# A two-layer hybrid encoder on one core: earlier weight loads, squares summed on VectorE, alternating output tiles, turned weights copied by ScalarE

## The chip, the core and the metric

The kernel runs on one core of a Trainium2 chip. The core has five engines with a queue each: PE (TensorE, matmuls and transposes), DVE (VectorE), ACT (ScalarE), POOL (GpSimd) and SP (SyncE, which here issues nearly all DMAs). PE writes its results to PSUM, which is handed out in banks of 128x512 float32; the other operands lie in SBUF. The metric is the device time of one execution in microseconds (us); less is better.

## The reference

Two layers over x of 512 tokens by 1024. Layer 0 mixes tokens by differential attention, layer 1 by chunked gated linear attention; both also attend to 256 tokens of memory with 4 heads, and each layer ends with a feed-forward part with a causal convolution of width 3.

```python
def rms_norm(x, g):
    xf = x.astype(jnp.float32)
    y = xf * lax.rsqrt(jnp.mean(xf * xf, axis=-1, keepdims=True) + EPS)
    return (y * g.astype(jnp.float32)).astype(x.dtype)
...
def memory_cross_attention(q, mem, mem_norm_g, w_kv, qk_norm_g):
    ...
    kv = rms_norm(mem, mem_norm_g) @ w_kv
    k, v = jnp.split(kv, 2, axis=-1)
    ...
    logits = jnp.einsum('bqhd,bkhd->bhqk', q, k).astype(jnp.float32)
    p = jax.nn.softmax(logits, axis=-1)
    o = jnp.einsum('bhqk,bkhd->bqhd', p.astype(v.dtype), v)
    return o.reshape(B, S, MEM_WIDTH)

def conv_ffn(h, w_up, conv_w, conv_b, w_down):
    u = h @ w_up
    c = lax.conv_general_dilated(u, ...) + conv_b
    a, g = jnp.split(c, 2, axis=-1)
    return (jax.nn.silu(g) * a) @ w_down
...
    for i in range(DEPTH):
        h = rms_norm(x, attn_norm[i])
        ...
        mix = diff_attention(...)   or   gla_attention(...)
        cross = memory_cross_attention(mem_q, mem, mem_norm[i], w_mem_kv[i], mem_qk_norm[i])
        x = x + jnp.concatenate([mix, cross], axis=-1) @ w_out[i]
        h = rms_norm(x, ffn_norm[i])
        x = x + conv_ffn(h, w_up[i], conv_w[i], conv_b[i], w_down[i])
    return x
```

## The kernel before

**Precision.** Every product of two float32 matrices is made of three matmuls in the faster format fp32r. Each operand is split in a high part (`xh`, `whi`: rounded to fp32r by ACT) and a low part (`xl`, `wlo`: what the rounding lost, by DVE); the products high x high, high x low and low x high add up in one PSUM bank. So each block of weights costs one ACT cast (`split_weights`, L199) and one DVE difference (L200), and each tile of activations one ACT scaling (L226) and one DVE instruction (L227).

**Weights.** All weights are packed in the order of their use into "pieces" of one or more blocks of 128 x up to 1024 (512 KB). `make_piece` (L202) loads a block into one of three `raw` buffers and splits it into one of five `whi` and five `wlo` buffers (WB). `weights(key)` (L216) hands out the next piece and makes pieces until the one after it is also made.

**Activations.** x is held transposed as eight tiles of 128 x 512, one for each 128 of the 1024 features (KT = 8; k counts them). A pool of 40 tiles of that size (`xtile`) serves all intermediate results. PSUM has four tags (`mm`, `sm`, `lg`, `tp`) with two banks each. A bank can be taken again only when the engine that reads its result is done.

**Order.** PE runs in program order. The start block (L336 to L395) also fixes the order of ACT, DVE, POOL and SP by hand; elsewhere a scheduler places the instructions of these four. Each engine works its queue off strictly in order, so an instruction that waits holds up all behind it. SP's DMAs go over eight lanes in turn; a DMA waits until the one eight places before it has landed.

**The start.** Eight times a tile of x and half a block of weights are loaded; `operands(k)` splits them and sums the squares of x (`squares`, L322: ACT squares, the sum is added by POOL, the last one by DVE). The first product (queries and keys of the first heads, `("qk", 0)`) takes them as they come, 12 matmuls for each k into four banks (L391 to L395). At k = 4 two small matmuls make the rows of the relative bias (`bias_rows`, copied to `bs` by DVE, L307). At k = 6 `weights` is called, which makes the second piece of four blocks (issues its loads, casts and differences); `token_rsqrt` forms the norm from the summed squares by a small matmul (L332), a logarithm and an exponential on ACT, and a Newton step on DVE (L175 to L177); then come the loads of constants, memory (`memT`), the vector of column factors (`cols`) and others. After the start, `small_vectors` scales seven of the columns on DVE (L400 to L403). The results of the first product are scaled out of PSUM by ACT (`qs`, `ks`, L539 and L540), and PE goes on with the second piece (L243 to L245).

**Attention with memory.** `MemAttn` runs in both layers beside the token mixer. For each of 8 units (4 token blocks x 2 halves of the heads): logits (L470), the negated maximum on DVE (L473), the exponential on ACT (L477), `turn` (four PE transposes into a `tp` bank, copied to SBUF by DVE, L487), `values` (L499). In layer 0 these steps lie in slots between the units of the differential attention, and matmuls of the big products (`Filler`) fill the gaps in PE's order.

**Out-projection.** `PASS` (L36) lists parts; each part is a list of (column block c, feature tiles ks). A column block is 256 wide and gives two output tiles 2c and 2c+1 (n = 0, 1). `unit` (L933) issues three matmuls for each ks into an `mm` bank; after the last, `update` (L922) adds the bank to x on DVE (L923); in the last part of a layer it also splits the new x for the feed-forward part and sums its squares (POOL, the last by DVE). In the last part of layer 0, blocks 2 and 3 have four ks (12 matmuls a tile), blocks 0 and 1 two (6 matmuls); their order is 2, 0, 1, 3.

**Feed-forward.** For each q, `up` (L954) makes four products: up and gate weights, n = 0 and 1; each sums over all eight k in their natural order (`product`, L255). DVE and ACT do the convolution (L961) and the gate. `("dn", ...)` goes back to 1024, again through `update`; at the end of layer 0 that also splits and sums squares.

Of the kernel before, what the change touches and what calls it, by code (L numbers as in the profile page):

```python
# [20 lines left out]
KT = D // 128  # L21
# [9 lines left out]
WB = 5  # L31
# [5 lines left out]
         [(2, (6, 7, 4, 5)), (0, (4, 5)), (1, (4, 5)), (3, (6, 7, 4, 5))]],  # L37
# [90 lines left out]
def trunk(ctx, tc, x_t, mem_t, wpack, cols_a_d, cols_d, conv_d, gate_d, rel_bias, diff_lambda, consts, onehot, out):  # L128
# [73 lines left out]
    def make_piece():  # L202
        parts = []
        for _, _, kk, _, w in blocks[len(made)]:
            n = len(kk)
            raw = wp.tile([128, WTILE], F32, name="raw", tag="raw", bufs=3)[:, :n * w]
            hi, lo = (wp.tile([128, WTILE], F32R, name=t, tag=t, bufs=WB)[:, :n * w] for t in ("whi", "wlo"))
            nc.sync.dma_start(raw, wpack[at[0], :, :n * w])
            split_weights(slice(0, n * w), raw, hi, lo)
            at[0] += 1  # L210
            parts += [(hi[:, blk(j, w)], lo[:, blk(j, w)]) for j in range(n)]
        made.append(parts)
# [42 lines left out]
    def product(p, parts, n, pairs, ids=None):  # L255
        for i in range(len(parts)) if ids is None else ids:
            (hi, lo), (bh, bl) = parts[i], pairs[i]
            mm(p, hi[:, blk(n)], bh, start=i == 0, stop=False)  # L258
            mm(p, hi[:, blk(n)], bl, start=False, stop=False)  # L259
            mm(p, lo[:, blk(n)], bh, start=False, stop=i == len(parts) - 1)  # L260
# [41 lines left out]
    def bias_rows(rb, oh, bs):  # L302
        for c in (slice(0, 512), slice(512, 640)):
            n = c.stop - c.start
            p = bank("lg")
            mm(p[:6, :n], rb, oh[:, c], start=True, stop=True)
            V.tensor_copy(bs[:, c], p[:6, :n])  # L307
# [14 lines left out]
    def squares(src, acc, on_dve):  # L322
        sq = xtile()
        A.activation(sq, src, AF.Square)
        if acc[0] is not None:
            (V if on_dve else G).tensor_add(sq, sq, acc[0])
        acc[0] = sq
# [7 lines left out]
    E = mybir.EngineType  # L335
    with tc.tile_pool(name="ini", bufs=1) as ip, tc.manual_schedule(engines={E.Activation, E.DVE, E.Pool, E.SP}):  # L336
# [3 lines left out]
        bs = ip.tile([6, 640], F32, name="bs")  # L340
        lv = perm.tile([128, 256], F32, name="lv")
        load = nc.sync.dma_start
# [15 lines left out]
        load(oh, onehot)  # L358
        parts, acc, split_w = [], [None], [None]
        made.append(parts)  # L360

        def operands(k):
            if k % 2 == 0:
                split_w[0] = [wp.tile([128, WTILE], F32R, name=n, tag=n, bufs=WB) for n in ("whi", "wlo")]
            c = blk(k % 2, S)
            hi, lo = split_w[0]
            xh[k], xl[k] = split_tiles()
            split(xh[k], xl[k], xT[k], c_attn(0, k))
            split_weights(c, raws[k // 2], hi, lo)
            parts.append((hi[:, c], lo[:, c]))  # L370
            squares(xT[k], acc, k == KT - 1)

        operands(0)
        for k in range(KT):
            if k + 1 < KT:
                operands(k + 1)
            if k == 4:
                bias_rows(rb, oh, bs)
            if k == KT - 2:
                weights(("qk", 0))  # L380
                token_rsqrt("lg", acc[0], NB, r_x[:, 0])
                load(bias_d, bs)
                load(C[:, 0:640], consts[:, 0:640])
                for i in range(4):
                    load(memT[i], mem_t[i])
                load(cols, cols_d)
                load(lv, diff_lambda[0].rearrange("a b -> (a b)").partition_broadcast(128))
                for l in range(2):
                    load(cv[l].rearrange("p a b -> p (a b)"), conv_d[l])
                load(gw, gate_d)  # L390
            hi, lo = parts[k]  # L391
            for b in range(NB):
                mm(first[b], xh[k][:, blk(b)], hi, start=k == 0, stop=False)
                mm(first[b], xh[k][:, blk(b)], lo, start=False, stop=False)
                mm(first[b], xl[k][:, blk(b)], hi, start=False, stop=k == KT - 1)  # L395

# [10 lines left out]
    def mem_squares():  # L407
        for i in range(4):
            squares(memT[i], mem_acc, False)
        sq = mem_acc[0]  # L410
        G.tensor_add(sq[:, 0:256], sq[:, 0:256], sq[:, 256:512])
# [35 lines left out]
    class MemAttn:  # L447
# [33 lines left out]
        def turn(self, u):  # L481
            pe, sm = self.live[u]
            pt = bank("tp")
            for t in range(4):
                transpose(pt[:, blk(t)], pe[:, blk(t)])
            pT = xtile()
            V.tensor_copy(pT, pt)  # L487
            self.live[u] = pT, sm
# [433 lines left out]
    def update(n, p, gain, acc):  # L922
# [5 lines left out]
        squares(xT[n], acc, n == KT - 1)  # L928

    def out_proj(l, mix, part, acc):  # L930
        got = {}

        def unit(c, ks, n, i):  # L933
            if i == 0:
                if n == 0:
# [6 lines left out]
        for c, ks in PASS[l][part]:  # L942
            for n in range(2):
                for i in range(len(ks)):
                    F.add(0.65, lambda c=c, ks=ks, n=n, i=i: unit(c, ks, n, i))

    def ffn(pool, l, acc):
# [4 lines left out]
        nu = [0]  # L952

        def up(parts, n):  # L954
# [3 lines left out]
            product(p, parts, n, list(zip(xh, xl)))  # L958
# [143 lines left out]
```

## Time and profile before

| | us |
|---|---|
| runs | 1226.18, 1223.9, 1224.32 (median 1224.32) |
| profiled execution | 1225.72 |
| its span | 1223.5 |
| PE busy | 1206.7 (99%) |
| DVE busy | 759.5 (62%) |
| ACT busy | 536.5 (44%) |
| POOL busy | 47.4 (4%) |
| summed squares on POOL (L326) | 42.0 in 27 instructions |
| differences of weights on DVE (L200) | 247.9 in 215 instructions |
| turned weights copied by DVE (L487) | 11.0 in 16 instructions |
| granted PE clock | 1.00 |

The profile describes one execution. The busy share of an engine is the time in which it had an instruction at work. In lists of single instructions the first two columns are start and duration in us; a bracket at the end gives the idle time of the engine before the instruction and the instruction that ended it ("<-DVE xt L923": it waited for DVE's instruction of line 923 that writes an `xt`). In the list of waits the columns are the waiting instruction, what it waited for, the sum in us, how often, and the longest. In the table of stretches each engine has its busy time and its count of instructions. Engine names with a q (SPq) are the queue itself, where a DMA is issued. A chain is followed back from the last instruction, at each step to what released it.

### The profile page before, as it was taken

The page shows a single profiled execution, that of the slowest core. Times are in us where ns is not written, and L with a number is a line of the kernel's source. Part 1 is how long each engine was busy: PE and PEld are TensorE (multiplying, and loading weights), DVE is VectorE, ACT ScalarE, POOL GpSimd, SP SyncE. Part 2 cuts the span into 40 slices and gives each one's busy share as a digit, 9 for nine tenths or more (in the row PEclk, how much of TensorE's full clock was granted, in tenths as well). Part 3 has the DMA queues.
Part 4 walks back from the last instruction along what each step waited for, and adds up shares of the span by engine and source line. Part 5 has one row for each costly group of instructions (what it writes and reads, how often), then busy time and mean ns, then how long its engine had stood idle before and what let it go on. Part 6 is the DMA issues. An engine that isn't in the chain of part 4 may idle for free.

```text
span 1223.5 us, 15052 instructions
## 1 busy us (share of the span) xinstructions
PE 1206.7 (99%) x5818; PEld 979.9 (80%) x5818; DVE 759.5 (62%) x1233; ACT 536.5 (44%) x901; POOL 47.4 (4%) x52
## 2 busy tenths in 40 slices
PE   9999999999999999999999999999999999999998
PEld 6777777778888888888887887888788888888887
DVE  6567578887777435777444436677867662376741
ACT  6666666554434213444436333435544332243420
POOL 3010000030000000000110000002100000000000
PEclk9999999999999999999999999999999999999999
DMA  6432231232322332323341221133323232232231
GB/s 234 145 106 95 78 113 52 70 119 71 105 102 86 103 104 87 103 85 104 114 130 52 69 70 57 40 121 129 104 69 118 89 106 88 83 113 94 83 116 43
DMA packets 39365, 117.76 MB, mean 96 GB/s; under 512 B 4679, under 2 KB 5720, under 8 KB 39294
## 3 DMA queue, kind: packets, MB, share of 16 engines
q1 hardware_dynamic: 39150, 116.79, 29.3%
q8 instruction: 45, 0.74, 0.2%
q14 instruction: 26, 0.21, 0.0%
q10 hardware_dynamic: 144, 0.02, 0.0%
HBM read 112.58 MB, written 4.21 MB: 95 GB/s over the span
## 4 chain that ended last, share of the span: by engine, by line
PE 90%; DVE 4%; ACT 2%; DMA 2%; issue 1%; SPq 0%; ACTq 0%; DVEq 0%
PE ps_mm L258 8%; PE ps_mm L259 8%; PE ps_mm L260 8%; PE ps_sm L258 7%; PE ps_sm L259 7%; PE ps_sm L260 6%; PE ps_mm L243 6%; PE ps_mm L245 6%; PE ps_mm L244 6%; PE ps_tp L258 3%; PE ps_tp L259 3%; PE ps_tp L260 3%; PE ps_lg L259 3%; PE ps_lg L260 3%; PE ps_lg L258 3%; PE ps_tp L168 2%
## 5 line engine op out<-in xcount | busy, mean ns | idle before, releaser
L199 ACT CAST whi<-raw 128x1024 fp32r<-128x1024 f32 (+4 forms) x215 | 209.2, 975 | 275.4 <-PE ps_tp L259 133.7
L200 DVE TENSOR_TENSOR wlo<-raw,whi 128x1024 fp32r<-128x1024 f32 (+4 forms) x215 | 247.9, 1155 | 119.7 <-ACT whi L199 115.9
L258 PE MATMUL ps_mm<-xsh,whi 128*128 128x512 f32 x480 | 190.7, 397 | 2.7 <-DVE xt L923 2.7
L259 PE MATMUL ps_mm<-xsl,whi 128*128 128x512 f32 x480 | 187.4, 390 | 0.0
L260 PE MATMUL ps_mm<-xsh,wlo 128*128 128x512 f32 x480 | 187.3, 390 | 0.0
L243 PE MATMUL ps_mm<-whi,xsh 128*128 128x512 f32 (+2 forms) x352 | 138.1, 392 | 2.7 <-ACT ks L540 2.7
L258 PE MATMUL ps_sm<-xsh,whi 128*128 128x512 f32 x352 | 137.1, 389 | 0.0
L260 PE MATMUL ps_sm<-xsh,wlo 128*128 128x512 f32 x352 | 137.0, 389 | 0.0
L259 PE MATMUL ps_sm<-xsl,whi 128*128 128x512 f32 x352 | 137.0, 389 | 0.0
L245 PE MATMUL ps_mm<-whi,xsl 128*128 128x512 f32 (+2 forms) x352 | 131.5, 374 | 0.3 <-DVE xsl L227 0.3
L244 PE MATMUL ps_mm<-wlo,xsh 128*128 128x512 f32 (+2 forms) x352 | 130.7, 371 | 0.0
L964 ACT ACTIVATE cvo<-u,cv 128x512 f32<-128x512 f32 x88 | 71.6, 814 | 121.3 <-DVE u L962 121.3
L258 PEld LDWEIGHTS ps_mm<-xsh,whi 128*128 128x128 f32 x480 | 90.2, 188 | 23.6 <-DVE xt L923 3.2
L260 PEld LDWEIGHTS ps_mm<-xsh,wlo 128*128 128x128 f32 x480 | 90.1, 188 | 19.0
L259 PEld LDWEIGHTS ps_mm<-xsl,whi 128*128 128x128 f32 x480 | 90.2, 188 | 18.6 <-DVE xsl L227 0.6
L965 DVE SCALAR_TENSOR_TENSOR cvo<-u,cv,cvo 128x512 f32<-128x512 f32 x88 | 65.9, 749 | 38.5 <-ACT cvo L964 38.5
L243 PEld LDWEIGHTS ps_mm<-whi,xsh 128*128 128x128 f32 x352 | 66.3, 188 | 17.6 <-issue 4.7
L260 PEld LDWEIGHTS ps_sm<-xsh,wlo 128*128 128x128 f32 x352 | 66.1, 188 | 13.7
L258 PEld LDWEIGHTS ps_sm<-xsh,whi 128*128 128x128 f32 x352 | 66.1, 188 | 13.7
L259 PEld LDWEIGHTS ps_sm<-xsl,whi 128*128 128x128 f32 x352 | 66.1, 188 | 13.6
L245 PEld LDWEIGHTS ps_mm<-whi,xsl 128*128 128x128 f32 x352 | 66.2, 188 | 12.8 <-DVE xsl L227 0.5
L244 PEld LDWEIGHTS ps_mm<-wlo,xsh 128*128 128x128 f32 x352 | 66.6, 189 | 9.4
(232 smaller groups left out, 1802.2 us busy)
## 6 DMA issues: line engine op xcount, KB each, us to landing
raw<-in_wpack_dram SPq DMA_DIRECT2D x176, 512.0 KB, 3.6
raw<-in_wpack_dram SPq DMA_DIRECT2D x28, 256.0 KB, 2.6
xt<-in_x_t_dram SPq DMA_DIRECT2D x16, 256.0 KB, 5.6
xres<-xt SPq DMA_DIRECT2D x8, 256.0 KB, 3.6
xt<-xres SPq DMA_DIRECT2D x8, 256.0 KB, 4.0
out_dram<-xt SPq DMA_DIRECT2D x8, 256.0 KB, 2.0
bt<-bias_d SPq DMA_DIRECT2D x6, 256.0 KB, 3.5
raw<-in_wpack_dram SPq DMA_DIRECT2D x4, 384.0 KB, 2.9
```

The source lines that it names most:

```text
L168: nc.tensor.transpose(dst, src, ident[:n, :n])
L199: A.copy(hi[:, c], raw[:, c])
L200: V.tensor_sub(lo[:, c], raw[:, c], hi[:, c].bitcast(F32))
L243: mm(p, sh[k][:, blk(b)], hi, start=k == 0, stop=False)
L244: mm(p, sh[k][:, blk(b)], lo, start=False, stop=False)
L245: mm(p, sl[k][:, blk(b)], hi, start=False, stop=k == KT - 1)
L258: mm(p, hi[:, blk(n)], bh, start=i == 0, stop=False)
L259: mm(p, hi[:, blk(n)], bl, start=False, stop=False)
L260: mm(p, lo[:, blk(n)], bh, start=False, stop=i == len(parts) - 1)
L964: A.activation(c, u[:, 2:], AF.Identity, scale=cv[l][:, 2, j:j + 1], bias=cv[l][:, 3, j:j + 1])
L965: V.scalar_tensor_tensor(c, u[:, 1:S + 1], cv[l][:, 1, j:j + 1], c, op0=ALU.mult, op1=ALU.add)
```

## The change

Five things are changed.

1. At the start, the loads of the second piece's four blocks are issued directly behind those of the first: three into the `raw` buffers, the fourth into the start's own buffer `raws[0]` after k = 0 has been read from it. `make_piece` then takes the buffers that it is given. The loads of constants, memory and columns stand behind the start block and outside the order by hand, as does what follows them; only the store of the bias rows stays in it, in two parts from two tiles.
2. All sums of squares are added by DVE: at the start, for the memory (L407), in the out-projections, and at the end of layer 0's feed-forward part.
3. The last part of layer 0's out-projection takes blocks in the order 2, 0, 3, 1, and `tiles` gives the output tiles in the order 4, 0, 5, 1, 6, 2, 7, 3: a tile of 12 matmuls, then one of 6.
4. The products of layer 0's up-projection sum over k in the same order; layer 1 keeps the natural one.
5. `turn` copies with ACT where DVE did.

```diff
@@ -34,7 +34,7 @@
 C4 = tuple(range(4))
 
 PASS = ([[(c, (0, 1)) for c in C4], [(c, (2, 3)) for c in C4], [(c, (6, 7)) for c in (0, 1)],
-         [(2, (6, 7, 4, 5)), (0, (4, 5)), (1, (4, 5)), (3, (6, 7, 4, 5))]],
+         [(2, (6, 7, 4, 5)), (0, (4, 5)), (3, (6, 7, 4, 5)), (1, (4, 5))]],
         [[(c, (0, 1, 2, 6, 7)) for c in C4], [(c, (3, 4, 5)) for c in C4]])
 
 
@@ -199,15 +199,21 @@
         A.copy(hi[:, c], raw[:, c])
         V.tensor_sub(lo[:, c], raw[:, c], hi[:, c].bitcast(F32))
 
-    def make_piece():
+    def raw_tile():
+        return wp.tile([128, WTILE], F32, name="raw", tag="raw", bufs=3)
+
+    def load_raw(raw, n):
+        nc.sync.dma_start(raw[:, :n], wpack[at[0], :, :n])
+        at[0] += 1
+        return raw
+
+    def make_piece(raws=None):
         parts = []
-        for _, _, kk, _, w in blocks[len(made)]:
+        for i, (_, _, kk, _, w) in enumerate(blocks[len(made)]):
             n = len(kk)
-            raw = wp.tile([128, WTILE], F32, name="raw", tag="raw", bufs=3)[:, :n * w]
-            hi, lo = (wp.tile([128, WTILE], F32R, name=t, tag=t, bufs=WB)[:, :n * w] for t in ("whi", "wlo"))
-            nc.sync.dma_start(raw, wpack[at[0], :, :n * w])
+            raw = load_raw(raw_tile(), n * w) if raws is None else raws[i]
+            hi, lo = (wp.tile([128, WTILE], F32R, name=t, tag=t, bufs=WB) for t in ("whi", "wlo"))
             split_weights(slice(0, n * w), raw, hi, lo)
-            at[0] += 1
             parts += [(hi[:, blk(j, w)], lo[:, blk(j, w)]) for j in range(n)]
         made.append(parts)
 
@@ -253,11 +259,13 @@
 
 
     def product(p, parts, n, pairs, ids=None):
-        for i in range(len(parts)) if ids is None else ids:
+        ids = range(len(parts)) if ids is None else ids
+        first, last = (ids[0], ids[-1]) if len(ids) == len(parts) else (0, len(parts) - 1)
+        for i in ids:
             (hi, lo), (bh, bl) = parts[i], pairs[i]
-            mm(p, hi[:, blk(n)], bh, start=i == 0, stop=False)
+            mm(p, hi[:, blk(n)], bh, start=i == first, stop=False)
             mm(p, hi[:, blk(n)], bl, start=False, stop=False)
-            mm(p, lo[:, blk(n)], bh, start=False, stop=i == len(parts) - 1)
+            mm(p, lo[:, blk(n)], bh, start=False, stop=i == last)
 
 
     xT = [None] * KT
@@ -304,7 +312,7 @@
             n = c.stop - c.start
             p = bank("lg")
             mm(p[:6, :n], rb, oh[:, c], start=True, stop=True)
-            V.tensor_copy(bs[:, c], p[:6, :n])
+            V.tensor_copy(bs[c.start // 512], p[:6, :n])
 
     def lam(lv, lp):
         l2 = small("l2")[:, :2]
@@ -319,11 +327,11 @@
     memT = [xtile() for _ in range(4)]
     first = [bank("mm"), bank("mm"), bank("sm"), bank("sm")]
 
-    def squares(src, acc, on_dve):
+    def squares(src, acc):
         sq = xtile()
         A.activation(sq, src, AF.Square)
         if acc[0] is not None:
-            (V if on_dve else G).tensor_add(sq, sq, acc[0])
+            V.tensor_add(sq, sq, acc[0])
         acc[0] = sq
 
     def token_rsqrt(tag, sq, nb, y, on_dve=False):
@@ -333,13 +341,13 @@
         return rsqrt(p[:, :nb], nb, 1.0 / D, on_dve, y=y)
 
     E = mybir.EngineType
+    load = nc.sync.dma_start
     with tc.tile_pool(name="ini", bufs=1) as ip, tc.manual_schedule(engines={E.Activation, E.DVE, E.Pool, E.SP}):
         idle = ip.tile([128, 512], F32, name="idle")
         rb = ip.tile([32, 6], F32, name="rb")
         oh = ip.tile([32, 640], F32, name="oh")
-        bs = ip.tile([6, 640], F32, name="bs")
+        bs = xtile()[:6], xtile()[:6, :128]
         lv = perm.tile([128, 256], F32, name="lv")
-        load = nc.sync.dma_start
         A.dma_start(cols_a, cols_a_d)
         G.memset(idle, 0.0)
         p = bank("tp")
@@ -356,6 +364,7 @@
         load(C[:, 640:768], consts[:, 640:768])
         load(rb, rel_bias)
         load(oh, onehot)
+        second = [load_raw(raw_tile(), WTILE) for _ in range(3)]
         parts, acc, split_w = [], [None], [None]
         made.append(parts)
 
@@ -368,31 +377,36 @@
             split(xh[k], xl[k], xT[k], c_attn(0, k))
             split_weights(c, raws[k // 2], hi, lo)
             parts.append((hi[:, c], lo[:, c]))
-            squares(xT[k], acc, k == KT - 1)
+            squares(xT[k], acc)
 
         operands(0)
         for k in range(KT):
             if k + 1 < KT:
                 operands(k + 1)
+            if k == 0:
+                second.append(load_raw(raws[0], WTILE))
             if k == 4:
                 bias_rows(rb, oh, bs)
             if k == KT - 2:
+                make_piece(second)
                 weights(("qk", 0))
                 token_rsqrt("lg", acc[0], NB, r_x[:, 0])
-                load(bias_d, bs)
-                load(C[:, 0:640], consts[:, 0:640])
-                for i in range(4):
-                    load(memT[i], mem_t[i])
-                load(cols, cols_d)
-                load(lv, diff_lambda[0].rearrange("a b -> (a b)").partition_broadcast(128))
-                for l in range(2):
-                    load(cv[l].rearrange("p a b -> p (a b)"), conv_d[l])
-                load(gw, gate_d)
+                for c in range(2):
+                    load(bias_d[:, 512 * c:min(512 * c + 512, 640)], bs[c])
             hi, lo = parts[k]
             for b in range(NB):
                 mm(first[b], xh[k][:, blk(b)], hi, start=k == 0, stop=False)
                 mm(first[b], xh[k][:, blk(b)], lo, start=False, stop=False)
                 mm(first[b], xl[k][:, blk(b)], hi, start=False, stop=k == KT - 1)
+
+    load(C[:, 0:640], consts[:, 0:640])
+    for i in range(4):
+        load(memT[i], mem_t[i])
+    load(cols, cols_d)
+    load(lv, diff_lambda[0].rearrange("a b -> (a b)").partition_broadcast(128))
+    for l in range(2):
+        load(cv[l].rearrange("p a b -> p (a b)"), conv_d[l])
+    load(gw, gate_d)
 
     def small_vectors():
         lam(lv, xtile()[:, 0:128].rearrange("p (a b) -> p a b", a=2))
@@ -406,9 +420,9 @@
 
     def mem_squares():
         for i in range(4):
-            squares(memT[i], mem_acc, False)
+            squares(memT[i], mem_acc)
         sq = mem_acc[0]
-        G.tensor_add(sq[:, 0:256], sq[:, 0:256], sq[:, 256:512])
+        V.tensor_add(sq[:, 0:256], sq[:, 0:256], sq[:, 256:512])
 
 
     def mem_kv(l):
@@ -484,7 +498,7 @@
             for t in range(4):
                 transpose(pt[:, blk(t)], pe[:, blk(t)])
             pT = xtile()
-            V.tensor_copy(pT, pt)
+            A.copy(pT, pt)
             self.live[u] = pT, sm
 
         def values(self, u):
@@ -925,24 +939,31 @@
             return
         xh[n], xl[n] = split_tiles()
         split(xh[n], xl[n], xT[n], gain(n))
-        squares(xT[n], acc, n == KT - 1)
+        squares(xT[n], acc)
+
+
+    def tiles(l, part):
+        cs, kk = [c for c, _ in PASS[l][part]], dict(PASS[l][part])
+        if l == 0 and part == 3:
+            return [2 * c + n for a in (0, 2) for n in range(2) for c in cs[a:a + 2]], kk
+        return [2 * c + n for c in cs for n in range(2)], kk
 
     def out_proj(l, mix, part, acc):
         got = {}
 
         def unit(c, ks, n, i):
             if i == 0:
-                if n == 0:
+                if c not in got:
                     got[c] = weights(("o", l, part, c))
                 got["p"] = bank("mm")
             p = got["p"]
             product(p, got[c], n, [mix[k] for k in ks], (i,))
             if i == len(ks) - 1:
                 update(2 * c + n, p, None if acc is None else (lambda k: c_ffn(l, k)), acc)
-        for c, ks in PASS[l][part]:
-            for n in range(2):
-                for i in range(len(ks)):
-                    F.add(0.65, lambda c=c, ks=ks, n=n, i=i: unit(c, ks, n, i))
+        todo, kk = tiles(l, part)
+        for n in todo:
+            for i in range(len(kk[n // 2])):
+                F.add(0.65, lambda n=n, i=i: unit(n // 2, kk[n // 2], n % 2, i))
 
     def ffn(pool, l, acc):
         rB = pool.tile([128, S], F32, name="rB", bufs=1)
@@ -950,12 +971,13 @@
         for u in us:
             G.memset(u[:, 0:2], 0.0)
         nu = [0]
+        order = tiles(l, len(PASS[l]) - 1)[0]
 
         def up(parts, n):
             i = nu[0]
             nu[0] += 1
             p = bank("mm" if i % 4 < 2 else "sm")
-            product(p, parts, n, list(zip(xh, xl)))
+            product(p, parts, n, list(zip(xh, xl)), order)
             return p, us[i % 4]
 
         def conv(p, u, j):
```

## The prediction

> **What bounds the kernel now.** I read the page first (busy shares, then the chain that ended last), then the list of waits for PE, then a table of stretches, and last the order of single instructions wherever PE waits.
>
> ```profile
> span 1223.5 us, 15052 instructions
> PE 1206.7 (99%) x5818; PEld 979.9 (80%) x5818; DVE 759.5 (62%) x1233; ACT 536.5 (44%) x901; POOL 47.4 (4%) x52
> PE 90%; DVE 4%; ACT 2%; DMA 2%; issue 1%; SPq 0%; ACTq 0%; DVEq 0%
> ```
>
> PE is busy for 1206.7 of 1223.5 us and holds 90% of the chain. The change leaves PE the same matmuls, so what it can win lies in the 16.8 us in which PE is idle; what it can lose has no such bound, because every us by which an operand comes late is a us of the end.
>
> ```profile
> PE ps_mm L258 <- DVE xt L923: 2.7, 3, 1.0
> PE ps_mm L243 <- ACT ks L540: 2.7, 1, 2.7
> PE ps_tp L168 <- DVE xt L487: 1.1, 1, 1.1
> PE ps_sm L499 <- DVE xt L487: 0.9, 1, 0.9
> ```
>
> These four waits (7.4 us: sum, number, longest) are the ones that the change touches directly: three waits for the add of the out-projection (L923), one at the start for the first keys, two for the copy of the turned weights (L487).
>
> ```profile
> 0.00:31.60 31.60, 29.88 (x114) 20.95 (x114) 22.01 (x24) 18.67 (x29) 9.53 (x11) 1.00 0.70 239
> 31.60:60.00 28.40, 25.72 (x128) 20.97 (x128) 13.73 (x44) 17.50 (x42) 0.29 (x2) 1.00 0.39 134
> 150.00:250.00 100.00, 96.67 (x584) 77.11 (x583) 78.66 (x206) 57.68 (x159) 0.14 (x1) 1.00 0.24 77
> 276.00:608.00 332.00, 331.95 (x1460) 273.63 (x1459) 208.79 (x258) 131.32 (x162) 4.42 (x3) 1.00 0.31 97
> 838.00:866.00 28.00, 26.99 (x118) 21.21 (x117) 23.14 (x27) 18.78 (x26) 11.29 (x10) 1.00 0.35 114
> ```
>
> Columns: stretch, length, busy time of PE, PEld, DVE, ACT, POOL, granted clock, DMA share, GB/s. The feed-forward stretch 276 to 608 has no idle PE at all; 331.95/1460 gives 0.227 us per 128x512 matmul, the unit of all that follows. The gaps are at the start, in the attention with memory (150 to 250) and around the out-projections.
>
> **The start.** Rows of SP, POOL, DVE and PE, then three of the chain, then the bandwidth of the first 36 us in 40 slices:
>
> ```profile
> 12.59 13.00 SPq L208 DMA_DIRECT2D raw<-in_wpack_dram  x4
> 15.13 3.24 POOL L326 TENSOR_TENSOR xt<-xt 128x512 f32<-128x512 f32 x2 [0.17 <-ACT xt L324]
> 9.01 1.38 DVE L227 SCALAR_TENSOR_TENSOR xsl<-xt,cols_a,xsh 128x512 fp32r<-128x512 f32 x1 [0.33 <-ACT xsh L226]
> 17.14 1.78 DVE L200 TENSOR_TENSOR wlo<-raw,whi 128x512 fp32r<-128x512 f32 x1
> 19.50 0.68 DVE L200 TENSOR_TENSOR wlo<-raw,whi 128x512 fp32r<-128x512 f32 x1
> 20.10 0.87 DVE L307 COPY bs<-ps_lg 6x512 f32<-6x512 f32 x2
> 23.43 0.67 DVE L326 TENSOR_TENSOR xt<-xt 128x512 f32<-128x512 f32 x1
> 24.03 3.48 DVE L200 TENSOR_TENSOR wlo<-raw,whi 128x1024 fp32r<-128x1024 f32 x3
> 30.85 1.23 DVE L200 TENSOR_TENSOR wlo<-raw,whi 128x1024 fp32r<-128x1024 f32 x1 [3.35 <-ACT whi L199]
> 33.87 0.27 DVE L400 TENSOR_SCALAR cols<-cols 128x1 f32<-128x1 f32 x3 [0.61 <-DMA cols<-in_cols_dram]
> 18.30 1.24 PE L306 MATMUL ps_lg<-oh,rb 32*6 32x512 f32 x4
> 13.95 5.73 DMA raw<-in_wpack_dram
> 25.26 4.41 DMA raw<-in_wpack_dram
> 34.32 0.50 PE ps_mm L243
> GB/s 0 2 216 369 180 269 330 316 323 396 401 410 401 389 394 356 308 319 405 401 364 46 0 0 0 0 0 0 18 141 348 304 217 328 394 369 289 200 329 378
> ```
>
> The fourth block of the second piece is issued only at 25.26, when DVE has read the first of the three raw buffers; it takes 4.41 us, and cast, difference, root and evacuation follow it until PE goes on at 34.32 after 2.7 us of idleness. The changed kernel reads that block into a start buffer, behind the third (issued at 13.95, landed at 13.95 + 5.73 = 19.7). At the 400 GB/s of the row its 512 KB take 1.3 us, so it lands at about 21.0. Squares added by DVE cost 0.67 less 0.07 of overlap, 0.60 each, but DVE's differences fall from 1.78 to 0.68 once POOL adds nothing beside them.
>
> That would be the whole 2.7, were it not for the order of DVE. Seven scalings of the columns vector (L400 to L403 of before) now stand in DVE's queue behind the square add of k=5 and ahead of the bias rows' copies and of all operands of k=6 and 7. DVE gets there early: from 9.0, where it starts on k=2, four steps of 1.86 (0.66 + 0.60 + 0.60) and the left-over add bring it to about 17. But the columns' load stands on SP behind the fourth block and the 320 KB of constants: 21.0 + 0.8 + a few tenths for the small transfer itself, T = 22.2. From T: 0.5 for the scalings, 0.8 for the copies, 2 x 1.86 for the operands, which makes T + 5.0 = 27.2 for the last square add. PE waits for that add with the product for the root, which stands ahead of the matmuls of k=6 and 7. It comes there after the bias rows (19.5 in before) and 24 matmuls (5.4), at 24.9 less the half us that POOL's neighbourhood cost before that: 24.3, so it waits about 3. The four differences of the second piece (3.48/3 = 1.16 each) end at T + 9.7 = 31.9; in before the last one ended at 32.1 and PE went on 2.2 later, so now at 34.1. Against 34.32 this is -0.2. The stall moves from behind the first product to its middle, and the end follows T one for one. Bounds: with T early enough not to matter PE does not wait at 24.3 and has 6.0 of work to the end of the first product, 30.3, which is -4.0; T = 24 gives +1.6. The columns' load in before waits 0.61 behind the other transfers; that speaks for a T with the queue, and I take 22.2. The memory tiles and the next weights are issued earlier than before, the bias rows go out in two stores behind DVE's copies; their readers have 10 us, so nothing is added.
>
> PE would stand idle for some 3 us. In before it stood for 2.7, and the granted clock in the stretch from 31.6 is 1.00; I add nothing, with 24 x 0.227 = 5.4 as the upper bound (the matmuls of k=6 and 7 at half rate).
> [...]
>
> **The squares of memory.** Four adds move from POOL to DVE in 60 to 150, where PE has under 1 us of waits and none for DVE's sums: 0, bounds -0.3 and +0.3.
>
> **The out-projections.** PE with its wait, DVE in two stretches, and the mean of the add:
>
> ```profile
> 259.29 0.50 PE L258 MATMUL ps_mm<-xsh,whi 128*128 128x512 f32 x1 [0.72 <-DVE xt L923]
> 263.33 0.50 PE L258 MATMUL ps_mm<-xsh,whi 128*128 128x512 f32 x1 [0.98 <-DVE xt L923]
> 260.88 1.79 DVE L227 SCALAR_TENSOR_TENSOR xsl<-xt,cols,xsh 128x512 fp32r<-128x512 f32 x1
> 263.20 0.74 DVE L227 SCALAR_TENSOR_TENSOR xsl<-xt,cols,xsh 128x512 fp32r<-128x512 f32 x1
> 854.20 2.31 DVE L200 TENSOR_TENSOR wlo<-raw,whi 128x1024 fp32r<-128x1024 f32 x1
> ```
>
> In layer 0 the last part has tiles of 12 matmuls (2.72 us) and of 6 (1.36). Per tile DVE has the add 0.60, the low half 0.66 and now the square add 0.60, 1.86 in all, and four differences of 1.16. Two short tiles in a row give DVE 2.72 for 3.72 of work, so PE waits for a bank: 0.72 and 0.98 above. Long and short in turn give 4.08 for 3.72, plus a difference now and then. Followed tile by tile, one wait of 0.9 is left, before the last tile, and the first product of the feed-forward ends at 273.1 instead of 274.5: -1.4. Bounds: both waits gone -1.9; if DVE falls behind by the seven adds (4.2) less the four differences of 1.1 that POOL stretched (1.79 against 0.74) +0.5.
>
> In layer 1 all tiles are alike (9 matmuls, 2.05 us) and the order stays. DVE is busy for 23.1 of 28 us there; seven adds bring 7 x 0.60 = 4.2, and the rows that POOL stretched (2.31 for 1.16 among them) give back about 3.4. DVE needs 1.86 per tile and half a difference of 1.16, 2.4 against PE's 2.05, so PE waits three times for 0.5 to 0.9 where it waited once for 1.0: +1.0, bounds -0.8 and +1.5.
>
> **The turned weights on ACT.** Layer 0, then layer 1, then the nearest row for such a copy on ACT:
>
> ```profile
> 193.74 0.68 DVE L487 COPY xt<-ps_tp 128x512 f32<-128x512 f32 x1
> 194.48 0.66 PE L168 MATMUL ps_tp<-C,ks 128*128 128x128 f32 x4 [1.08 <-DVE xt L487]
> 194.98 0.21 ACT L477 ACTIVATION_READ_ACCUMULATOR xt<-ps_lg,nmm 128x1 f32 x1
> 675.33 1.00 PE L499 MATMUL ps_sm<-vm,xt 128*128 128x64 f32 x8
> 676.03 1.05 ACT L199 CAST whi<-raw 128x1024 fp32r<-128x1024 f32 x1
> 679.06 1.11 PE L499 MATMUL ps_sm<-vm,xt 128*128 128x64 f32 x8 [0.90 <-DVE xt L487]
> L612 ACT COPY xt<-ps_tp 128x512 f32<-128x512 f32 x6 | 3.5, 579 | 0.0
> ```
>
> A copy costs 0.58 on ACT, 0.68 on DVE; what counts is what stands ahead of it. At 194 it is now behind the four exponentials, which end at 195.1: the copy ends at 195.7, PE's keys start then and not at 194.48: +1.2. At 208 a weight cast of 0.6 has moved between the exponentials: +0.5. DVE, 79% busy from 150 to 250, loses eight copies (4.8), from which I expect back 0.6 in the small waits there. In layer 1 the first copy stands behind two casts: it begins at 676.03 + 0.95 = 677.0 and ends at 677.6. Its reader, in before at 675.33, waits 2.3; the wait of 0.90 at 679.06 has its operand early then and goes: +1.4. The other copies come in time by the same reckoning, two of them just so. Sum +2.5; bounds -2.0 (both waits for L487 gone, nothing in their place) and +4.0.
>
> **The sum.** -0.2 + 0 - 1.4 + 1.0 + 2.5 = +1.9. The profiled execution took 1225.72 us, of which 1223.5 are its span, so 1227.6 by its own time. The runs are 1226.18, 1223.9 and 1224.32; the median 1224.32 lies 1.4 under the profiled one, and against it the forecast is 1226.2.
>
> **The rivals.**
> A, faster: the columns land early or PE's wait for them is short, and ACT takes the copies without being late. Start -2, out-projections -1.4 and 0, copies -0.4 (between -2 and +1.2): -3.8, 1220.5. For it: DVE is the busier engine in every stretch with waits, and all four waits quoted go. Against it: the orders of DVE and ACT described above.
> B, slower: T is 24 (+1.8 over the forecast), because the small columns transfer waits as it did in before (0.61 behind its neighbours, 5.3 after its issue at 28.59), or the clock falls in PE's longer idle time. 1228.0. From T = 22.8 on it passes the 0.2% named below.
> C, slower: weights of layer 0's feed-forward come late.
>
> ```profile
> L965 DVE SCALAR_TENSOR_TENSOR cvo<-u,cv,cvo 128x512 f32<-128x512 f32 x88 | 65.9, 749 | 38.5 <-ACT cvo L964 38.5
> ```
>
> Its products take k in the alternated order too, so they need both blocks of a piece at their beginning and hold both to the end. Of five buffers four are live; the time from a freed block to its need falls from two products to one, 24 x 0.227 = 5.4 us. Cast 1.05, difference 1.16 and four of DVE's convolution steps ahead of them (4 x 0.75) make 5.2, just inside. One step more is 0.5 per group of four products, times 11 groups 5.5: 1231.7. Against it: PE loses 0.05 us in 332 now.
>
> **How the numbers follow.** Forecast 0.44, its own range 1224.4 to 1228.0; A 0.30; B 0.14; C 0.12. A difference under 0.2% (1221.9 to 1226.8) can't be told from none. Faster: most of A, 0.27. Slower: B, C and a third of the forecast's case, 0.40. Same: the rest, 0.33. The range reaches to the middle of A and short of C: 1220.5 to 1230.0.
>
> **What would show it.** Start: the DVE row of the first column scaling with a wait for its DMA, ending near 22.2, and PE waiting about 3 us for the last square add, with ks L540 no more among the waits. Out-projection: waits for L923 in layer 0 fall to one, in layer 1 rise to three. Copies: the waits for L487's successor on ACT of 2.3 at 194 and 2.3 at 675. Feed-forward: 332 us with 0 to 0.1 idle, or C is right. The forecast fails if the scalings don't wait, or if ACT's copies end before 194.5 and 675.3.

## The result, and the profile after

The changed kernel takes 1233.9 us (median of five executions, 1231.01 to 1236.94), the kernel before 1225.55 beside it (1223.9 to 1227.06). The ratio is 1.0073, 95% interval 1.006 to 1.0087: 8.35 us slower by the medians, where 1.9 were forecast and the range ended at 1230.0. The profiled execution took 1236.94 and is the slowest of the five; this has to be kept in mind when its numbers are added up. The kernel before, timed again beside the experiments, has medians of 1224.72, 1224.85 and 1226.15 there, so a difference between medians of two experiments can be off by about 1 us.

The page of the changed kernel, its waits for PE, and its stretches (columns as before):

```profile
span 1235.2 us, 15019 instructions
PE 1214.0 (98%) x5818; PEld 984.9 (80%) x5818; DVE 749.6 (61%) x1245; ACT 545.5 (44%) x917; POOL 4.6 (0%) x24
```
```profile
PE ps_lg L340 <- DVE xt L334: 3.0, 1, 3.0
PE ps_sm L513 <- ACT xt L501: 3.0, 2, 2.1
PE ps_mm L266 <- DVE xt L937: 2.5, 5, 0.7
PE ps_tp L168 <- ACT xt L501: 2.3, 1, 2.3
PE ps_lg L601 <- ACT xt L491: 1.6, 4, 0.8
```
```profile
0.00:31.60 31.60, 27.28 (x96) 19.44 (x97) 20.15 (x37) 18.97 (x29) 0.73 (x5) 0.92 0.81 277
31.60:60.00 28.40, 28.40 (x136) 23.06 (x136) 11.17 (x34) 15.56 (x37) 0.29 (x2) 0.97 0.22 74
150.00:250.00 100.00, 94.78 (x564) 75.81 (x562) 68.82 (x185) 59.70 (x162) 0.29 (x2) 0.97 0.21 71
276.00:608.00 332.00, 331.39 (x1454) 272.45 (x1453) 209.42 (x263) 130.46 (x162) 0.00 (x0) 1.00 0.29 97
640.00:710.00 70.00, 66.42 (x372) 53.01 (x370) 26.41 (x59) 36.04 (x84) 0.53 (x1) 0.98 0.21 71
```

The waits for ks L540 (2.7) and for DVE's copies (1.1 and 0.9) are gone, and in their place stand waits of 3.0 at the start, of 2.3 in layer 0 and of 2.1 and 0.9 in layer 1. But for the 0.9, that was the forecast. What was not in its sum is the column of the granted clock: 0.92 and 0.97 at the start, 0.97 and 0.98 in the stretches with the other long waits; before, it was 1.00 in all of these. And PE's busy time rose by 7.3 us for the same 5818 matmuls. So part of the time went not into waiting but into slower matmuls. Two of the three places, in PE's order:

```profile
27.37 1.86 PE L340 MATMUL ps_lg<-C,xt 128*128 128x1 f32 x8 [3.02 <-DVE xt L334]
29.09 0.77 PE L398 MATMUL ps_mm<-whi,xsh 128*128 128x512 f32 x1
29.67 0.63 PE L399 MATMUL ps_mm<-wlo,xsh 128*128 128x512 f32 x1
30.09 0.63 PE L400 MATMUL ps_mm<-whi,xsl 128*128 128x512 f32 x1
...
33.51 0.40 PE L399 MATMUL ps_sm<-wlo,xsh 128*128 128x512 f32 x1
33.74 0.39 PE L400 MATMUL ps_sm<-whi,xsl 128*128 128x512 f32 x1
```
```profile
684.47 1.11 PE L513 MATMUL ps_sm<-vm,xt 128*128 128x64 f32 x8 [2.07 <-ACT xt L501]
685.41 1.03 PE L168 MATMUL ps_tp<-C,xt 128*128 128x128 f32 x4
686.10 0.78 PE L249 MATMUL ps_mm<-whi,xsh 128*128 128x512 f32 x1
686.67 0.63 PE L250 MATMUL ps_mm<-wlo,xsh 128*128 128x512 f32 x1
687.10 0.63 PE L251 MATMUL ps_mm<-whi,xsl 128*128 128x512 f32 x1
```

Behind the wait of 3.02 the matmuls start 0.42 to 0.43 us apart (29.67, 30.09) instead of 0.227, until 33.5. Behind the 2.07 us of idle time in layer 1 it is the same (686.67, 687.10).

### The profile page after: what moved, and what is told of

It reads as the page before. It is cut to its first block, busy times and chain, and to the rows that moved or that the text cites. A ratio compares the mean times of both kernels' runs of the same rounds, so it can differ in the third digit from the quotient of the medians.

```text
span 1235.2 us, 15019 instructions
## 1 busy us (share of the span) xinstructions
PE 1214.0 (98%) x5818; PEld 984.9 (80%) x5818; DVE 749.6 (61%) x1245; ACT 545.5 (44%) x917; POOL 4.6 (0%) x24
## 4 chain that ended last, share of the span: by engine, by line
PE 89%; DVE 4%; ACT 3%; DMA 2%; issue 1%; SPq 0%; ACTq 0%; DVEq 0%
PE ps_mm L266 8%; PE ps_mm L267 8%; PE ps_mm L268 8%; PE ps_sm L266 6%; PE ps_sm L267 6%; PE ps_sm L268 6%; PE ps_mm L249 6%; PE ps_mm L251 6%; PE ps_mm L250 6%; PE ps_tp L266 3%; PE ps_tp L267 3%; PE ps_tp L268 3%; PE ps_lg L267 3%; PE ps_lg L268 3%; PE ps_lg L266 3%; PE ps_tp L168 2%
## 5 line engine op out<-in xcount | busy, mean ns | idle before, releaser
L200 DVE TENSOR_TENSOR wlo<-raw,whi 128x1024 fp32r<-128x1024 f32 (+4 forms) x215 | 240.2, 1128 | 111.7 <-ACT whi L199 108.1
```

The costliest lines, as they stand in the source:

```text
L200: V.tensor_sub(lo[:, c], raw[:, c], hi[:, c].bitcast(F32))
```

## The experiments

The executions of all kernels, sorted (how many, where not all are listed); at the end of a line the granted clock of the fastest and the slowest:

```
changed kernel           1231.01 1232.39 1233.9 1236.54 1236.94                  (0.999, 0.993)
loads back               1226.4, nine from 1228.28 to 1229.04, 1231.2            (1.0, 0.996)
copies by DVE            1226.94 to 1229.23 (11)                                 (0.999, 0.996)
both                     1221.39 to 1222.53 (6)                                  (1.0, 0.999)
matmuls at the start     1230.28 1231.04 1231.47 1231.48 1233.0                  (1.0, 0.997)
matmuls in layer 0       1225.55 1225.78 1225.93 1228.46 1228.48 1228.7 1229.0   (1.0, 0.997)
natural order            1222.05 to 1223.2 (11)                                  (1.0, 1.0)
POOL in layer 1          1220.73 to 1222.1 (7)                                   (1.0, 1.0)
ACT copies in layer 0    1223.25 to 1224.99 (11)                                 (1.0, 0.999)
matmuls in all waits     1229.7 to 1230.19 (6)                                   (1.0, 1.0)
before, with matmuls     1223.63 to 1224.62 (11)                                 (0.999, 1.0)
before, beside it        1223.11 to 1227.36 (17)                                 (1.0, 0.997)
```

**1. The loads put back.** In the changed kernel the loads of constants, memory and columns return into the start block, behind the store of the bias rows:

```diff
                 for c in range(2):
                     load(bias_d[:, 512 * c:min(512 * c + 512, 640)], bs[c])
+                load(C[:, 0:640], consts[:, 0:640])
+                for i in range(4):
+                    load(memT[i], mem_t[i])
+                load(cols, cols_d)
...
-    load(C[:, 0:640], consts[:, 0:640])
-    for i in range(4):
-        load(memT[i], mem_t[i])
-    load(cols, cols_d)
...
```

> The changed kernel with the loads of constants, memory and columns put back where before.py had them, so that the columns' scalings no longer stand ahead of the bias rows' copies and the last operands on DVE. Theory (the idle time of PE lowers its clock): the wait of 3.0 us for the last square add goes, and with it the stretch at half rate that follows it (15 matmuls 0.427 apart instead of 0.227, 2.6 us with the root's product): PE reaches the second piece at about 30.5 instead of 36.7, the granted clock up to 60 us is 1.00, and the time falls by about 6 from that of the changed kernel, to about 1228. Rival (the low clock comes of itself, whatever PE does): only the wait goes, about -3, 1231, and the matmuls behind it still run 0.427 apart. Rival (the wait moves on, to the fourth block of the second piece or the root): less than -2.

1228.82 (ratio to before 1.0029, 1.002 to 1.0038), 5.1 less than the changed kernel. Wait and low clock at the start are both gone (its stretches):

```profile
0.00:31.60 31.60, 30.30 (x117) 21.96 (x118) 21.05 (x41) 21.35 (x37) 0.73 (x5) 1.00 0.88 296
31.60:60.00 28.40, 28.40 (x144) 22.83 (x142) 15.05 (x37) 18.23 (x41) 0.29 (x2) 1.00 0.30 100
150.00:250.00 100.00, 94.56 (x556) 75.24 (x555) 74.04 (x197) 60.17 (x163) 0.14 (x1) 0.97 0.23 76
```

PE reaches the second piece at 31.13 instead of 36.71. That the wait sat where it did because of the columns, the trace of the changed kernel shows on DVE; the second row is the first scaling:

```profile
15.02 0.69 DVE L334 TENSOR_TENSOR xt<-xt 128x512 f32<-128x512 f32 x1
22.29 0.28 DVE L414 TENSOR_SCALAR cols<-cols 128x1 f32<-128x1 f32 x3 [6.58 <-DMA cols<-in_cols_dram]
```

**2. The copies by DVE again.**

```diff
-            A.copy(pT, pt)
+            V.tensor_copy(pT, pt)
```

> The changed kernel with the turned weights copied by DVE again. Theory: the ACT copies cost their waits (2.3 at 197.7, 2.1 at 684.5, 1.0 at 695) less the two waits of before (1.1 and 0.9) and the half clock behind the first two (2.6 and 1.5): -6 to -7 from the changed kernel, 1227 to 1228, with clock 1.00 from 150 to 250 and from 640 to 710, and the low clock at the start alone. Rival (only queue order, the clock is not connected): -2.5 as in the sum of the prediction, 1231.5, with a clock under 1 in the same two stretches.

1228.27 (1.0023, 1.0014 to 1.0032): 5.6 less, nearer to the theory's 6 to 7 than to 2.5. The clock is 1.00 from 150 to 250 and from 640 to 710 and stays low at the start alone (0.95 and 0.99).

**3. Both edits.**

> Both edits: loads back at their place, copies by DVE. What is left of the change is the early loads of the second piece, the squares on DVE and the alternated tiles. Theory: no wait over 1.1 us, clock 1.00 throughout, start -4, out-projections -1.1 and +1.0: about 1220.5, faster than both kernels. Rival (something else of the change costs, the feed-forward's order of k or the squares): 1224 or more.

1221.75 (0.9971, 0.9959 to 0.9982), faster than the kernel before by some 3 us. PE reaches the second piece at 29.95 (34.32 before). With both edits 12.2 go, with each alone 5.1 and 5.6, 10.7 together: the two causes lie beside each other, and what the sum leaves open is 1.5.

**4. Matmuls in the wait at the start.** This and three more kernels leave a wait as it is and give PE something to do in it; their additional results are not read.

```diff
+                pz = bank("tp")
+                for _ in range(12):
+                    mm(pz, xh[0][:, blk(0)], parts[0][0], start=True, stop=True)
                 token_rsqrt("lg", acc[0], NB, r_x[:, 0])
```

> The changed kernel with 12 more 128x512 matmuls whose results nobody reads, put on PE into the wait of 3.0 us ahead of the root's product. The wait for the last square add stays, PE is idle for only 0.3 us of it. Theory (idle time lowers the clock): the matmuls behind run 0.227 apart, granted clock 1.00 from the start to 60 us, PE at the second piece by about 34.1 instead of 36.7, -2.6: about 1231.3. Rival (the clock falls of itself, or by load): the matmuls behind still run 0.427 apart, the time stays at 1234.

1231.47 (1.0049, 1.0037 to 1.0062), as the theory had it. In its trace the twelve matmuls stand in the wait, and those that follow start 0.23 apart:

```profile
24.28 2.88 PE L395 MATMUL ps_tp<-whi,xsh 128*128 128x512 f32 x12
27.00 0.97 PE L340 MATMUL ps_lg<-C,xt 128*128 128x1 f32 x8
...
28.38 0.40 PE L403 MATMUL ps_mm<-whi,xsl 128*128 128x512 f32 x1
28.61 0.39 PE L401 MATMUL ps_mm<-whi,xsh 128*128 128x512 f32 x1
...
33.65 0.50 PE L249 MATMUL ps_mm<-whi,xsh 128*128 128x512 f32 x1
```

More work on PE made the kernel 2.4 us faster by the medians; the intervals of the two ratios just overlap, so the distances of the matmuls are the stronger evidence. The second piece starts at 33.65; the forecast, without the clock, was 34.1.

**5. Matmuls in the wait of layer 0**, on top of the first experiment:

```diff
+                if h == 5 and nm == "kT":
+                    pz = bank("mm")
+                    for _ in range(9):
+                        mm(pz, mix[0][0][:, 0:128], mix[0][0], start=True, stop=True)
```

> The first experiment's kernel (loads back, copies by ACT) with 9 more 128x512 matmuls, unread, on PE between the queries' and the keys' transposes of the sixth head, where PE waits 2.3 us for the ACT copy. The wait stays, PE is idle for 0.3 us of it. Theory (idle time lowers the clock): the clock from 150 to 250 us goes from 0.97 to 1.00, the instructions behind the wait run at their usual distances, -2.6: about 1226.2. Rival (ACT's late copy alone costs, the slow instructions behind it have another cause): 1228.8 unchanged.

1228.46 (1.0021, 1.0007 to 1.0035): the median hardly moved, so this expectation failed. The single executions say why: three at 1225.55 to 1225.93 with clock 1.0, four at 1228.46 to 1229.0 with 0.997 or 0.998. Only layer 1's long wait is left unfilled here, so by times and clocks it is behind this wait that the clock falls in some executions and not in others; the profiled execution is one of the three without a fall. By the same measure most executions of the first experiment lost 2.5 once, one none, and the profiled one twice, as its stretches show (0.97 above, and 0.98 from 640 to 710).

**6. Without the alternated order**, from the third experiment's kernel: the blocks in order 2, 0, 1, 3, both tiles of a block in turn, k in natural order.

```diff
-        if l == 0 and part == 3:
-            return [2 * c + n for a in (0, 2) for n in range(2) for c in cs[a:a + 2]], kk
...
-        order = tiles(l, len(PASS[l]) - 1)[0]
+        order = range(KT)
```

> The third experiment's kernel (loads back, copies by DVE) without the alternated order: the last part of layer 0's out-projection in blocks 2, 0, 1, 3 with both tiles of a block in turn, and the up-projection over k in natural order, squares still on DVE. Theory: two short tiles in a row give DVE 3.7 of work in 2.7 us, PE waits for banks twice as before or more: PE enters the up-projection 1.5 to 2.5 later, about 1223.7. Rival (the alternated k costs in the feed-forward what it brings here): the stretch from 276 to 608 loses 0.6 of idle time, the time stays within 0.5 of 1221.75.

1222.6 (0.9985, 0.9976 to 0.9994), 0.85 more than the third. Its two waits against the one that the third experiment has in the same place:

```profile
255.02 0.50 PE L266 MATMUL ps_mm<-xsh,whi 128*128 128x512 f32 x1 [1.32 <-DVE xt L937]
259.27 0.50 PE L266 MATMUL ps_mm<-xsh,whi 128*128 128x512 f32 x1 [1.24 <-DVE xt L937]
```
```profile
258.99 0.50 PE L266 MATMUL ps_mm<-xsh,whi 128*128 128x512 f32 x1 [0.71 <-DVE xt L937]
```

The waits are 1.85 longer (1.32 + 1.24 - 0.71), but a part comes back later: matmul by matmul the third experiment is ahead by 1.5 after the out-projection and by 0.7 from layer 0's second down-projection on, where it has two waits that this kernel has not. So the alternation is worth less than expected, and the rival is half right.

**7. Layer 1's squares on POOL**, from the third's kernel (`squares` and `update` take `on_dve`, false in layer 1 but for the last tile):

```diff
-            V.tensor_add(sq, sq, acc[0])
+            (V if on_dve else G).tensor_add(sq, sq, acc[0])
```

> The third experiment's kernel with the squares of layer 1's out-projection summed by POOL again (the last by DVE), as before. Theory: DVE has 7 adds less there, PE's waits fall from three (0.5, 0.9, 0.7) to the one of about 1.0, -1.0: about 1220.7, the best of all. Rival (DVE's rows stretched by POOL cost as much as the adds): no change, 1221.75.

1221.06 (0.9968, 0.9957 to 0.998), the lowest median of all. PE waits once instead of three times, for 1.02 at 852.94, and takes 0.67 less from the second piece to its last matmul (1184.75 against 1185.42). Against the third experiment's 1221.75 the intervals overlap.

**8. ACT's copies in layer 0 alone**, from the third's kernel: `(A.copy if self.l == 0 else V.tensor_copy)(pT, pt)`.

> The third experiment's kernel with the turned weights copied by ACT in layer 0 alone. Theory: the wait at the sixth head's keys goes from 1.1 to 2.3 and brings the half clock (2.6), some 0.7 and 0.4 follow at the next logits: +4.5 to +5, about 1226.5, and what is missing to the first experiment's 1228.8 is layer 1's share, 2 to 3. Rival (the costs are equal per copy): +3.5, 1225.3.

1223.72 (0.9991, 0.9982 to 1.0): +2.0, below both. The wait of 2.3 is there, but the clock stayed at 0.999 to 1.0 in all eleven executions: eight lie from 1223.25 to 1223.87, and the three with 0.999, from 1224.6 to 1224.99, may have lost a little. So the copies of layer 0 cost their waits, 1.75 from the second piece to PE's last matmul (1187.18 against 1185.42). Layer 1's cost 2.4 by the same measure (1189.62, the profiled execution of the fifth experiment, also with clock 1.00, against 1187.18). Of the 7.1 between the third and the first experiment that leaves 2.9 for the clock; in which layer it was lost, the times do not say.

**9. Matmuls in all three long waits** of the changed kernel (12, 9, and 8 ahead of the second unit's values in layer 1).

> The changed kernel with unread 128x512 matmuls on PE in all three long waits: 12 at the start, 9 at the sixth head's keys in layer 0, 8 ahead of the second unit's values in layer 1. All waits stay. Theory (the spread and part of the loss are the clock that falls behind idle time, in some executions and not in others): granted clock 1.00 in every execution, the times within 1.5 of each other, about 1230.4, the fastest of what the executions of the fourth experiment showed (1230.28 at clock 1.0). So 3.5 of the change's loss is clock and the rest is waits. Rival (the spread has another cause): a spread of 3 or more remains, median 1231.5.

1229.75 (1.0035, 1.0023 to 1.0047), all six executions within 0.5, where the changed kernel's five lie 6 apart. Its stretches of 150 to 250 and 640 to 710:

```profile
150.00:250.00 100.00, 96.65 (x582) 76.76 (x581) 73.96 (x197) 60.87 (x164) 0.14 (x1) 1.00 0.24 76
640.00:710.00 70.00, 68.76 (x378) 54.72 (x377) 23.11 (x43) 36.29 (x85) 0.52 (x1) 1.00 0.17 53
```

**10. The kernel before, with ten matmuls in its wait of 2.7 us.**

> The kernel before with 10 more 128x512 matmuls, unread, in its own idle time of 2.7 us ahead of the second piece. Theory: the kernel before also lost clock in some executions (0.996 to 1.0); with the idle time filled its times keep to the lower end, 1223.2 to 1224, median about 1.0 lower than the kernel before's, clock 1.00 throughout. Rival (2.7 us of idle time never cost the kernel before any clock): same median and the same spread.

1224.22 against 1226.15 for the kernel before in the same runs (0.9988, 0.9979 to 0.9996), within 1.0 against 4.3 (1223.11 to 1227.36). The kernel before lost clock behind its idle time too, in some executions (granted clock 0.997 to 1.0, with the matmuls 0.999 or 1.0); its profiled one, with 1.00 throughout, was not one of them.

## Why the prediction was wrong

From the medians: 1233.9 - 1229.75 = 4.2 us of the changed kernel are clock. The ninth against the tenth experiment, both with clock 1.00, leaves 1229.75 - 1224.22 = 5.5 for waits, where 1.9 were forecast. The kernel before had about 0.5 to 2 of clock loss itself, 1.3 by its median of 1225.55. So of the 6.4 by which the sum was too low, 2.8 are clock (4.15 - 1.33), a term that it put at nothing, and 3.6 are waits: 1.9 for the copies, 0.9 for the out-projections and what follows them, both worked out below, and 0.8 that stays open; the start alone differs by more between executions of one start block (29.84 to 31.13 in the experiments with the loads put back).

**The clock, the first step that failed.** The prediction saw that PE would stand idle for 3 us, put 5.4 down as the upper bound for a slower clock and took nothing, because the profiled execution of before had stood idle for 2.7 with 1.00 behind it. That was one execution; the spread of the three on record, 1223.9 to 1226.18, left room for others, and the tenth experiment shows that there were. In the trace of the changed kernel the granted clock is 0.50 from 27.4 to 33.3. In that profiled execution the start's share is 36.71 - 33.97 = 2.7 (the second piece's start there and in the ninth experiment; 3.1 against the fourth's 33.65). The further mistake was to ask this question at one wait only: for ACT's copies the same working had waits of 2.3 twice, and the clock was not asked about there. In the same trace it is 0.50 there too, from 197.4 to 204.1 at the end of the wait of 2.33 us, and from 685.5 to 688.8 behind that of 2.07. From the second piece to PE's last matmul the profiled execution takes 1194.3, the ninth experiment 1189.8: 4.5 for these two.

**The start without the clock: right.** The scalings began at 22.29 (forecast T = 22.2), PE waited 3.02 (about 3), and with the wait filled PE is at the second piece at 33.65 to 33.97 (34.1). The bound for a start without the columns' wait, 30.3, is met in the six experiments with the loads put back: 29.84 to 31.13.

**The out-projections: right in place, a little small.** In layer 0 PE has one large wait left, 0.71 before the last tile, in layer 1 three (0.36, 0.70, 0.54). Compared matmul by matmul with the kernel before, the third experiment gains 0.45 between the second piece and the out-projection (forecast 0), 0.65 at layer 0's out-projection (1.4), and loses 0.8 at layer 1's (1.0). The upper bound of +0.5 for layer 0 does not come out of its own terms, 4.2 less four times 1.1, which is below nothing; the forecast does not use it. What the prediction did not have is 0.9 at the start of layer 0's second down-projection, 0.6 of it in two waits (rows of the changed kernel; in the sixth experiment, without the alternated order, these waits are missing):

```profile
588.11 0.50 PE L266 MATMUL ps_lg<-midh,whi 128*128 128x512 f32 x1 [0.38 <-ACT midh L1017]
588.84 0.51 PE L267 MATMUL ps_lg<-midl,whi 128*128 128x512 f32 x1 [0.23 <-DVE midl L1018]
```

All in all the third experiment takes 0.5 more than before from the second piece to the end (1185.42 against 1184.94), where -0.4 was forecast. Rival C is out: no product of the up-projections waits for weights.

**The copies, the second step: mechanism right, sum mis-sized.** The two waits came where they were said, for 2.33 (2.3) and 2.07 (2.3), behind the exponentials and behind two casts:

```profile
196.94 0.21 ACT L491 ACTIVATION_READ_ACCUMULATOR xt<-ps_lg,nmm 128x1 f32 x1
197.04 0.60 ACT L501 COPY xt<-ps_tp 128x512 f32<-128x512 f32 x1
682.88 1.05 ACT L199 CAST whi<-raw 128x1024 fp32r<-128x1024 f32 x1
683.82 0.60 ACT L501 COPY xt<-ps_tp 128x512 f32<-128x512 f32 x1
695.16 1.10 PE L513 MATMUL ps_sm<-vm,xt 128*128 128x64 f32 x8 [0.91 <-ACT xt L501]
```

But a copy that was to come "just so" came 0.91 too late (695.16), and the 0.6 that DVE's relief was to bring back did not come. The waits alone went up by 1.25 and 0.8 in layer 0 (forecast 1.2 and 0.5) and by 2.1 in layer 1 (1.4). From the second piece on, the ninth experiment takes 1189.79, the third 1185.42: 4.4 for the copies without clock, against 2.5.

**The chances.** A, the fast rival, fell at both of the conditions named for it; with the two edits of the third experiment it is what happens. B had the clock as its second possibility and its direction, at one place and with 1228.0 too low.

## What to carry to other kernels

Waits of 2.07 to 3.02 us on PE cost more than their length here in some executions: the granted clock went to 0.50 and the matmuls started 0.427 instead of 0.227 us apart. Ask behind each idle time of that size whether the matmuls after it still run at their distance, and read the granted clock of several executions, not of the profiled one alone. Work that nobody reads, put into the wait, told the two apart in one run (the fourth experiment: 0.23 apart, clock 1.00). Before an instruction is moved to a less busy engine, look at what stands ahead of it in that engine's queue at each of its sixteen places; and before a small load is issued earlier, look at which instruction waits for it and what is queued behind that one.

## What the runs showed of the hardware

In the profiled execution of the changed kernel the granted clock fell to 0.50 at idle times of PE of 3.02, 2.33 and 2.07 us: from 26.67 to 33.50, from 197.34 to 204.16 and from 685.44 to 688.86, that is for 6.83, 6.82 and 3.42 us. There 128x512 matmuls started 0.427 instead of 0.227 us apart: at the start from 29.1 to 33.3, in layer 0 from 202.2 to 203.9, in layer 1 from 686.7 to 688.4. It did not do so in every execution: behind layer 0's 2.3 us hardly or not at all in the eleven of the eighth experiment (clock 0.999 to 1.0), behind layer 1's 2.1 us in four of seven of the fifth (0.997 or 0.998 in the four, 1.0 in the three, by their times and clocks). With PE kept busy in these waits the executions of the changed kernel agreed within 0.5 us, all with clock 1.0.

Why the same wait costs in one execution and not in another was not shown. The length alone does not decide it: 2.07 us of layer 1 were enough in the changed kernel's profiled execution, but in other profiled executions idle times as long or longer left the clock at 1.00: the 2.3 us of layer 0 in those of the fourth and the eighth experiment (150 to 250), the 2.1 of layer 1 in that of the fifth (640 to 710), the 2.68 of the kernel before (31.6 to 60).
